# Moving projection steps from the middle of a recurrence to its end, in a hybrid RWKV-7 and latent-attention block

## The chip, the cores and the metric

The kernel runs on one core of a Trainium2 chip. The metric is the device time of one execution in microseconds; the comparison is between medians of several runs. PE is TensorE (PEld its weight loads), DVE VectorE, ACT ScalarE, POOL GpSimd and SP SyncE, which issues most DMAs.

## What is computed

One decoder layer over 1024 tokens of width 1024, all in float32. The input is normed and modulated, and one projection of 3360 columns feeds two groups. The first is an RWKV-7 recurrence of 8 heads of 64, the second a latent attention of 8 heads. Each result is multiplied by a gate from the same projection; both are joined, projected back, and added to the input. Cut to what matters:

```python
h = rms_norm(x, norm_g[l]) * (1 + scale[:, None, :]) + shift[:, None, :]
proj = h @ w_in[0]
y_rwkv, v_first = rwkv7_time_mix(proj[..., :SHIFT_WIDTH], ...)       # recurrence, then group norm per head
y_mla = mla_branch(proj[..., O_CQ:O_CKV], proj[..., O_CKV:O_KR], proj[..., O_KR:O_GM], ...)
y = concatenate([y_rwkv * silu(proj[..., O_GR:O_CQ]), y_mla * silu(proj[..., O_GM:])])
x = x + gate[:, None, :] * (y @ w_out[l])
return rms_norm(x, final_g)

def step(state, inp):                                                # of the recurrence
    sa = einsum('bhvk,bhk->bhv', state, kk_t)
    state = state * w_t - sa[..., None] * (kk_t * a_t) + v_t[..., None] * k_t
    y = einsum('bhvk,bhk->bhv', state, r_t)
```

## The kernel before

**Tiling.** Matrix products that need float32 accuracy are made of three matmuls, high by high, high by low and low by high, on operands split into a rounded part and a rest. The projection works in tiles of 128 output columns by 512 tokens; each takes 8 blocks of the contraction, three matmuls a block (`mm3`, L159 to L161). Such a block is one *step* of `proj` (L333), and a tile of 128 columns has 16 steps. Its results go through the two PSUM banks of `psM`.

**The recurrence** is cut into 8 units: 4 pairs of heads (p) by 2 halves of the sequence (h), each with 8 chunks of 64 tokens. For a unit, `prep` (L462) makes decayed keys, queries and values, `products` (L544) the products within a chunk, `invert` (L588) inverts the triangular matrices by 62 dependent operations on DVE and stores them through DRAM (`d_n`, `d_w`), `fetch` and `tmat` (L607, L621) build the matrix T. Then `chain` (L653) runs the 8 chunks in three slots each: X is copied by ACT (L672), T times X (L679) and the copied result go into ST (L685, L686), and the new state is written (L693, L694); Y collects the output (L676, L696). `post` (L700) is the group norm: a copy of Y (L705), a reduction (L707, L708), the subtraction on POOL (L709), squares on ACT (L712), a second reduction (L714, L715), the power and the product on POOL (L716, L717), transposes on PE (L723), the affine part on ACT (L726), and the sum, gate and store (L730 to L736).

**What sets the order.** A loop of 11 rounds (n = 0 to 10) weaves these together. Round n has STEPS[n] slots (j). It prepares unit n at the slots of PREP and PROD, builds T of unit n - 1, runs the chain of unit n - 2, one third of a chunk in each slot, and does the group norm of unit n - 3 in five pieces, at the slots of POST. In each slot RATE[n] is added to a debt, and for each whole unit of debt one step of the *filler* is issued. The filler (L913) goes through the 24 remaining projection tiles: keys, values and queries of the later units, the latents (`latent`, L349: three tiles for queries, two for keys and values), and the gates; then through `values` (L830), which makes the rotated queries (`qrope`), the value matrix Vt (L863 to L872) and keys and queries of the first head pair (`heads_qk`, L794). That is 428 steps in all. What the rounds leave is drained after the loop.

Two calls of `latents` (L818) load the projected latents back from DRAM and split them: the first one the query latents (SP issues them by L763, ACT and DVE split them), in round 7, the second one those of keys and values, in round 8. `values` starts only after both, and after all projections, because its tiles take the memory of the normed input.

The program is traced in this order; a scheduler then orders the instructions of each engine by priority, and each engine runs its own in that order. After the loop, attention begins with the scores (`scores`, L1013), whose first matmul is L1023.

Of the kernel before, what the change touches and what calls it, by code (L numbers as in the profile page):

```python
# [57 lines left out]
PREP = ((0, 0, 1, 2, 3, 5, 5, 7), (4, 4, 5, 6, 7, 9, 9, 11), (9, 9, 10, 11, 12, 14, 14, 16))  # L58
PROD = ((8, 13), (12, 15), (17, 21))
TURN = (2, 5, 6)  # L60
POST = (1, 1, 5, 5, 8)
TMAT = ((13, 15), (14, 15), (15, 17))
EVAC = 120
STEPS = (16, 16, 24, 24, 24, 24, 24, 24, 24, 24, 9)
RATE = (2.3, 2.3, 2, 2, 2.2, 2, 2, 2, 1.7, 0.4, 1)
SCALE = 96 ** -0.5

_COLS = [("c", 8), ("norm_g", 8), ("b_shift", 8), ("b_scale", 8), ("mu", 13), ("a0", 4), ("k_k", 4),
# [14 lines left out]
def hymba_kernel(ctx: ExitStack, tc: tile.TileContext, x, pos, cols, cst, winit, w_ada, b_gate, w_in, w_lora, w0,  # L83
# [460 lines left out]
    def products(un, q):  # L544

        p, h, kb, rq = un["p"], un["h"], un["kb"], un["rq"]
        pp = [psA.tile([P, 4, P], F32, tag="rp", name="gps") for _ in range(2)]
        for i in range(4):
            c = q * 4 + i
            for s in range(2):  # L550
                rows = slice(s * 64, s * 64 + 64)
                T.matmul(pp[s][:, i, :], lhsT=kb[rows, c, :, :].rearrange("p a t -> p (a t)"),  # L552
                         rhs=rq[rows, c, :, :].rearrange("p a t -> p (a t)"), start=True, stop=True)
        dn = d_n[2 * p + h][:].rearrange("(s q c b) i j -> s q b i c j", s=2, q=2, b=2)
        for s in range(2):
            mk = cs("m_b" if s else "m_a")
            ga = ch.tile([P, 4, P], F32, tag="GA", name="GA", bufs=CB["GA"])
            un["GA"][s][q] = ga
            V.tensor_tensor(ga[:], pp[s][:], mk[:, None, :].to_broadcast([P, 4, P]), ALU.mult)
            for b in range(2):  # L560
                rr = slice(s * 64 + b * 32, s * 64 + b * 32 + 32)
                SY.dma_start(dn[s, q, b], ga[rr, :, b * 32:b * 32 + 32])

    def alloc_b(un):
        un["KB"] = ch.tile([P, 2, 8, C], F32, tag="KB", name="KB", bufs=CB["KB"])
        un["ST"] = ch.tile([P, 8, 2, C], F32, tag="ST", name="ST", bufs=CB["ST"])

    def turn_kb(un):

        ps = [psA.tile([P, 8, C], F32, tag="rt", name="tps") for _ in range(2)]  # L570
        for c in range(8):
            for s in range(2):
                rows = slice(s * 64, s * 64 + 64)
                T.transpose(ps[s][:, c, :], un["kb"][rows, c, :, :].rearrange("p a t -> p (a t)"), ident[rows, rows])
        for s in range(2):
            A.activation(un["KB"][:, s], ps[s][:], AF.Copy, scale=col("hs_b" if s else "hs_a"))

    def turn_v(un, q):

        qs = slice(q * 4, q * 4 + 4)  # L580
        ps = psA.tile([64, 4, P], F32, tag="rt", name="vps")
        for i in range(4):
            c = q * 4 + i
            T.transpose(ps[:, i, :], un["v"][:, c * C:(c + 1) * C], ident)
        A.copy(un["ST"][64:128, qs, 0, :], ps[:, :, 0:64])
        A.copy(un["ST"][0:64, qs, 1, :], ps[:, :, 64:128])

    def invert(un):  # L588

        i = 2 * un["p"] + un["h"]  # L590
        N = ch.tile([P, 32, 32], F32, tag="N", name="N", bufs=CB["N"])
        for q in range(4):
            SY.dma_start(N[q * 32:(q + 1) * 32], d_n[i][:])
        W = ch.tile([P, 8, 32], F32, tag="W", name="W")
        SY.dma_start(W[:].rearrange("p i t -> p (i t)"), winit)
        tp = ch.tile([P, 128], F32, tag="wtmp", name="wtmp")
        for u in range(31):
            n, m = u // 4 + 1, 31 - u
            t = tp[:, :n * m].rearrange("p (i t) -> p i t", i=n)
            V.tensor_tensor(t, W[:, 0:n, u:u + 1].to_broadcast([P, n, m]),  # L600
                            N[:, u:u + 1, u + 1:32].to_broadcast([P, n, m]), ALU.mult)
            V.tensor_tensor(W[:, 0:n, u + 1:32], W[:, 0:n, u + 1:32], t, ALU.subtract)  # L602
        d = d_w[i][:].rearrange("n (i q) t -> q n i t", q=4)
        for q in range(4):
            SY.dma_start(d[q], W[q * 32:(q + 1) * 32])

    def fetch(un):  # L607

        i = 2 * un["p"] + un["h"]
        TT = un["TT"] = TTs[un["h"]]  # L610
        dw = d_w[i][:].rearrange("(s c b) i j -> s b i c j", s=2, b=2)
        W1 = ch.tile([P, 8, 32], F32, tag="W1", name="W1")
        T1 = un["T1"] = ch.tile([P, 8, 32], F32, tag="T1", name="T1")
        for s in range(2):
            a = s * 64
            SY.dma_start(W1[a:a + 32], dw[s, 0])
            SY.dma_start(TT[a + 32:a + 64, :, 32:64], dw[s, 1])
            SY.dma_start(TT[a:a + 32, :, 0:32], dw[s, 0])
            V.transpose(flat(T1)[a:a + 32], flat(W1)[a:a + 32])

    def tmat(un):  # L621

        GA, TT, T1 = un["GA"], un["TT"], un["T1"]
        ps = psA.tile([P, 8, 32], F32, tag="rt", name="y1ps")
        for c in range(8):
            for s in range(2):
                a = s * 64
                T.matmul(ps[a + 32:a + 64, c, :], lhsT=GA[s][c // 4][a:a + 32, c % 4, 32:64], rhs=T1[a:a + 32, c, :],
                         start=True, stop=True)
        Y1 = ch.tile([P, 8, 32], F32, tag="Y1", name="Y1")  # L630
        A.mul(Y1[32:64], ps[32:64], -1.0)
        V.tensor_scalar(Y1[96:128], ps[96:128], -1.0, None, ALU.mult)
        yield
        ps = psA.tile([P, 8, 32], F32, tag="rt", name="y2ps")
        for c in range(8):
            for s in range(2):
                a = s * 64
                T.matmul(ps[a:a + 32, c, :], lhsT=Y1[a + 32:a + 64, c, :], rhs=TT[a + 32:a + 64, c, 32:64],
                         start=True, stop=True)
        A.copy(TT[0:32, :, 32:64], ps[0:32])  # L640
        V.tensor_copy(TT[64:96, :, 32:64], ps[64:96])

        for q in range(2):
            A.copy(GA[0][q][0:64, :, 0:C], un["rq"][0:64, q * 4:q * 4 + 4, 0, :])
            A.copy(GA[1][q][64:128, :, 0:C], un["rq"][64:128, q * 4:q * 4 + 4, 0, :])
        yield
# [284 lines left out]
    def late(n):  # L931

        return 2 if 2 <= n <= 6 else int(n == 1)

    def after(n):

        at_ = {}

        def put(j, f):
            at_.setdefault(j, []).append(f)  # L940

        if n < 8:
            g = prep(units[n])
            for j in PREP[late(n)]:
                put(j, lambda g=g: next(g, None))
            for j, q in zip(PROD[late(n)], range(2)):
                put(j, lambda q=q: products(units[n], q))
            put(PROD[late(n)][1], lambda: invert(units[n]))
        if 1 <= n < 9:
            un = units[n - 1]  # L950
            put(0, lambda: alloc_b(un))
            put((1, 5, 11)[late(n - 1)], lambda: fetch(un))
            put(TURN[0], lambda: turn_kb(un))
            for j, q in zip(TURN[1:], range(2)):
                put(j, lambda q=q: turn_v(un, q))
            g2 = tmat(un)
            for j in TMAT[1 if n == 1 else late(n - 1) and 2]:
                put(j, lambda g2=g2: next(g2, None))
        if 3 <= n < 11:
            g3 = post(units[n - 3])  # L960
            for j in POST:
                put(j, lambda g3=g3: next(g3, None))
        return at_

# [3 lines left out]
    for n in range(11):  # L968
        at_ = after(n)
        rec = chain(units[n - 2], units[n - 1] if n % 2 == 0 else None) if 2 <= n < 10 else None  # L970
        for j in range(STEPS[n]):
            if rec is not None:
                next(rec, None)
            for f in at_.pop(j, ()):
                f()
            if (n, j) == (7, PREP[0][-1] + 1):
                next(la)
            if (n, j) == (8, TURN[2]):
                next(la)
                turned.append(1)  # L980
            debt += RATE[n]
            while debt >= 1:
                next(fill, None)
                debt -= 1
        assert not at_, at_.keys()
# [349 lines left out]
```

## Time and profile before

| what | us |
|---|---|
| median of three runs (lowest, highest) | 945.38 (942.20, 951.51) |
| the profiled execution: time; span from the first to the last instruction | 947.39; 945.6 |
| first X copies of the eight units, rounds 2 to 9 | 167.4, 228.6, 296.0, 358.1, 424.3, 493.7, 561.2, 606.6 |
| last projection matmul; first value matmul (L863) | 591.1; 607.6 |
| last Y matmul ends; last transposes L723; first scores L1023 | 648.3; 657.1; 664.7 |

How to read the views. A window row gives a stretch (start:end in us from the span's start), its length, the busy time and the number of instructions of PE, PEld, DVE, ACT and POOL, the share of the clock granted to PE, the mean busy share of the DMA engines, and GB/s. A row of waits gives who waited for whom, the sum in us, how many times, and the longest. A timeline row gives start, duration, engine, line, operation and operands; in brackets stands the idle time of its engine just before, and what ended it. A row of a group of instructions gives the line, the operation, its count, then busy us, mean ns of one, and idle time before. Matmuls overlap each other, so that a stream of them starts one more often than each lasts.

### The profile page before, as it was taken

Reading aid. Unit: us, or ns where it says so; the run is one execution under the profiler, and the core shown is the slowest. Engines: PE = TensorE matmul, PEld = TensorE weight load, DVE = VectorE, ACT = ScalarE, POOL = GpSimd, SP = SyncE. Lnnn points to the kernel's source line nnn. Section 1 sums busy time; section 2 is a strip of 40 time slices with the busy share of each in tenths; the row PEclk is TensorE's granted clock in tenths of the full one; section 3 lists DMA queues with packets and bytes.
Section 4 is the critical chain, followed back from the end, with each engine's and each line's share of the span. In section 5 each row is a group of like instructions: output and inputs, shape, how many; then the busy total and the mean of one; then the engine's idle time right before and its main releaser. Section 6 shows DMA issues by size and latency. Waiting matters only on the chain.

```text
span 945.6 us, 16387 instructions
## 1 busy us (share of the span) xinstructions
PE 850.4 (90%) x5828; PEld 638.6 (68%) x5828; DVE 576.5 (61%) x1438; ACT 476.7 (50%) x1132; POOL 294.1 (31%) x355
## 2 busy tenths in 40 slices
PE   1799998999889999999999899896899998989897
PEld 1587776776667567667776666663677777868685
DVE  5796484293863855936636736462678778764333
ACT  2656131535635535445435444564688788762311
POOL 2314131133222322412325130323346454464300
PEclk9999998799999999999999999797899999999899
DMA  8762313124413424232332543335202031026133
GB/s 270 228 183 73 84 29 87 57 68 107 143 37 98 138 68 124 72 81 86 90 85 63 140 123 87 113 103 150 54 26 71 26 101 57 1 89 223 56 115 130
DMA packets 116737, 93.01 MB, mean 98 GB/s; under 512 B 38952, under 2 KB 92464, under 8 KB 116656
## 3 DMA queue, kind: packets, MB, share of 16 engines
q1 hardware_dynamic: 115696, 88.82, 32.0%
q0 software_dynamic: 960, 3.15, 1.4%
q8 instruction: 46, 0.75, 0.3%
q14 instruction: 35, 0.29, 0.1%
HBM read 69.12 MB, written 22.81 MB: 97 GB/s over the span
## 4 chain that ended last, share of the span: by engine, by line
PE 54%; DVE 17%; ACT 9%; DMA 7%; issue 5%; POOL 5%; SPq 1%; POOLq 0%; DVEq 0%; ACTq 0%
PE mm L159 8%; PE mm L160 6%; PE mm L161 6%; DVE W L602 3%; DVE wtmp L600 3%; DMA wor<-in_w_out 2%; PE tp L1052 2%; ACT pr L1041 2%; PE gps L552 2%; PE po L1114 2%; PE po L1116 2%; PE po L1115 2%; PE Y L676 2%; ACT PTh L1061 1%; PE rc L668 1%
## 5 line engine op out<-in xcount | busy, mean ns | idle before, releaser
L159 PE MATMUL mm<-hTh,whi 128*128 128x512 f32 (+1 forms) x384 | 171.8, 447 | 1.9 <-DVE tg L230 1.9
L160 PE MATMUL mm<-hTl,whi 128*128 128x512 f32 (+1 forms) x384 | 154.2, 402 | 0.0
L161 PE MATMUL mm<-hTh,wlo 128*128 128x512 f32 (+1 forms) x384 | 154.2, 401 | 0.0
L152 POOL TENSOR_TENSOR wlo<-wraw,whi 128x512 fp32r<-128x512 f32 (+1 forms) x54 | 69.8, 1293 | 206.8 <-ACT whi L151 192.3
L159 PEld LDWEIGHTS mm<-hTh,whi 128*128 128x128 f32 (+1 forms) x384 | 72.3, 188 | 23.6 <-issue 2.3
L161 PEld LDWEIGHTS mm<-hTh,wlo 128*128 128x128 f32 (+1 forms) x384 | 72.3, 188 | 17.8
L160 PEld LDWEIGHTS mm<-hTl,whi 128*128 128x128 f32 (+1 forms) x384 | 72.8, 190 | 12.4 <-issue 1.4
L1045 POOL TENSOR_SCALAR pr<-pr,sm 128x512 f32<-128x512 f32 (+2 forms) x96 | 55.2, 584 | 77.4 <-DVE sm L1042 50.0
L602 DVE TENSOR_TENSOR W<-W,wtmp 128x60 f32<-128x60 f32 (+24 forms) x248 | 68.8, 277 | 6.0
L600 DVE TENSOR_TENSOR wtmp<-W,N 128x60 f32<-128x60 f32 (+24 forms) x248 | 66.1, 267 | 7.0 <-DMA N<-d_n 0.9
L1041 ACT ACTIVATE pr<-sp,mx,rss 128x128 f32<-128x128 f32 (+3 forms) x64 | 53.3, 833 | 15.4 <-DVE mx L1034 13.0
L1062 DVE TENSOR_TENSOR PTl<-tp,PTh 128x512 fp32r<-128x512 f32 (+2 forms) x96 | 52.4, 554 | 12.2 <-ACT PTh L1061 10.1
L151 ACT CAST whi<-wraw 128x512 fp32r<-128x512 f32 (+1 forms) x54 | 32.6, 605 | 51.6 <-PE mm L160 45.1
L1033 DVE TENSOR_REDUCE mx<-sp 128x1 f32<-128x128 f32 (+3 forms) x64 | 48.0, 750 | 13.4 <-PE sp L1027 13.3
L1114 PE MATMUL po<-wo,yh 128*128 128x512 f32 x128 | 51.7, 404 | 3.9 <-DVE xo L1247 3.1
L1061 ACT CAST PTh<-tp 128x512 fp32r<-128x512 f32 (+2 forms) x96 | 44.0, 477 | 14.4 <-PE tp L1052 10.6
L1115 PE MATMUL po<-wo,yh 128*128 128x512 f32 x128 | 51.2, 400 | 0.0
L1116 PE MATMUL po<-wo,yl 128*128 128x512 f32 x128 | 51.2, 400 | 0.0
L1052 PE MATMUL tp<-cstt,pr 128*128 128x128 f32 x288 | 44.9, 278 | 4.4 <-POOL pr L1045 2.1
L1073 PE MATMUL op<-PTh,Vt 128*128 128x256 f32 (+1 forms) x160 | 41.9, 292 | 5.1 <-ACT od L1088 5.1
L685 ACT ACTIVATE ST<-rc 64x64 f32<-64x64 f32 x64 | 13.8, 215 | 52.7 <-PE rc L682 44.7
L1023 PE MATMUL sp<-kt,qt 96*128 96x512 f32 (+2 forms) x96 | 36.4, 379 | 4.2 <-ACT pr L1041 4.2
(394 smaller groups left out, 1974.7 us busy)
## 6 DMA issues: line engine op xcount, KB each, us to landing
wraw<-in_w_in SPq DMA_DIRECT2D x52, 256.0 KB, 3.0
wa<-in_w_ada SPq DMA_DIRECT2D x64, 128.0 KB, 3.4
xt<-in_x SPq DMA_DIRECT2D x8, 512.0 KB, 5.8
wg<-in_w_ada SPq DMA_DIRECT2D x32, 128.0 KB, 2.2
N<-d_n SPq DMA_DIRECT2D x32, 128.0 KB, 2.8
wor<-in_w_out SPq DMA_DIRECT2D x16, 256.0 KB, 2.9
cr<-d_c SPq DMA_DIRECT2D x14, 256.0 KB, 2.8
d_c<-craw SPq DMA_DIRECT2D x10, 256.0 KB, 2.6
```

Source lines behind the costliest of these rows:

```text
L152: G.tensor_tensor(lo[:, :, :m], raw[:, :, :m], hi[:, :, :m].bitcast(F32), ALU.subtract)
L159: T.matmul(ps[:m], lhsT=hi[:, k % 4, :m], rhs=a, start=first, stop=False)
L160: T.matmul(ps[:m], lhsT=hi[:, k % 4, :m], rhs=b, start=False, stop=False)
L161: T.matmul(ps[:m], lhsT=lo[:, k % 4, :m], rhs=a, start=False, stop=last)
L600: V.tensor_tensor(t, W[:, 0:n, u:u + 1].to_broadcast([P, n, m]), N[:, u:u + 1, u + 1:32].to_broadcast([P, n, m]), ALU.mult)
L602: V.tensor_tensor(W[:, 0:n, u + 1:32], W[:, 0:n, u + 1:32], t, ALU.subtract)
L1041: A.activation(pr[:, 0:n], sp[:, 0:n], AF.Exp, scale=rss[:, i:i + 1], bias=mx[:], accum_out=sm[:])
L1045: G.tensor_scalar(pr[:, a:e], pr[:, a:e], sm[:], 1.0, ALU.mult, ALU.mult)
L1052: T.transpose(tp[:, j, :], pr[:, (j0 + j) * P:(j0 + j + 1) * P], ident)
L1114: T.matmul(ps, lhsT=yh[k][:, ts_], rhs=hi, start=first, stop=False)
L1115: T.matmul(ps, lhsT=yh[k][:, ts_], rhs=lo, start=False, stop=False)
L1116: T.matmul(ps, lhsT=yl[k][:, ts_], rhs=hi, start=False, stop=last)
```

## The change

Three tables of numbers and one slot are changed:

```diff
-POST = (1, 1, 5, 5, 8)
+POST = ((1, 1, 5, 5, 8), (0, 0, 9, 9, 13))
-STEPS = (16, 16, 24, 24, 24, 24, 24, 24, 24, 24, 9)
-RATE = (2.3, 2.3, 2, 2, 2.2, 2, 2, 2, 1.7, 0.4, 1)
+STEPS = (16, 16, 24, 24, 24, 24, 24, 24, 24, 24, 14)
+RATE = (2.3, 2.3, 1.8, 1.8, 1.9, 1.8, 1.8, 1.8, 1.75, 1.3, 1)
...
-            for j in POST:
+            for j in POST[n == 10]:
                 put(j, lambda g3=g3: next(g3, None))
...
-            if (n, j) == (7, PREP[0][-1] + 1):
+            if (n, j) == (7, 16):
                 next(la)
```

Rounds 2 to 7 issue fewer steps in a slot, round 9 more, and round 10, which holds only the last unit's group norm, has 14 slots instead of 9; that norm's transposes come at slot 9 and not 5. The query latents are loaded at slot 16 of round 7 and not at slot 8.

In the built order this moves instructions at three places. On PE, from the last Y matmul of the last unit (L696) on: `ytps` are the norm's transposes, `vps` value blocks, `qkps` keys and queries of the first head pair. Before:

```order
L696 MATMUL Y<-ST,GA 64x64 x2
L787 MATMUL qkps<-ckvh_6000,wkl 128x512
L723 MATMUL ytps<-cstt,ys 64x128 x8
L785 MATMUL qkps<-cqh_5411,wqh 128x512
L786 MATMUL qkps<-cql_5414,wqh 128x512
L787 MATMUL qkps<-cqh_5411,wql 128x512
```

With the change (four value blocks and a rotated query's block stand where the dots are):

```order
L696 MATMUL Y<-ST,GA 64x64 x2
L863 MATMUL vps<-wvh,ckvh_5868 128x512
L864 MATMUL vps<-wvl,ckvh_5868 128x512
...
L864 MATMUL vps<-wvl,ckvh_5869 128x512
L865 MATMUL vps<-wvh,ckvl_5871 128x512
L723 MATMUL ytps<-cstt,ys 64x128 x8
L785 MATMUL qkps<-ckvh_5868,wkh 128x512
L786 MATMUL qkps<-ckvl_5870,wkh 128x512
```

33 matmuls of 512 columns stand between the last Y matmul and the transposes, where one stood, and 30 between the transposes and the first scores, where 18 stood.

On DVE, between the two reductions of the last unit's norm (L707 and L714). Before:

```order
L707 TENSOR_REDUCE s_6599<-ys 128x8
L805 TENSOR_TENSOR kt_6648<-qkps,kt_6648 64x512
L708 TENSOR_SCALAR s_6599<-s_6599 128x8
L753 TENSOR_TENSOR wkl<-wkr,wkh 128x128 x2
L805 TENSOR_TENSOR kt_6648<-qkps,kt_6648 64x512
L714 TENSOR_REDUCE s_6605<-y_6603 128x8
```

With the change:

```order
L707 TENSOR_REDUCE s_6549<-ys 128x8
L872 TENSOR_TENSOR Vt<-vps,Vt 128x4x128
L436 TENSOR_TENSOR rl<-q_6515,rh 128x512
L708 TENSOR_SCALAR s_6549<-s_6549 128x8
L424 STREAM_SHUFFLE rot<-q_6575 128x512
L431 TENSOR_TENSOR q_6575<-q_6575,tabs 128x512
L431 TENSOR_TENSOR rot<-rot,tabs 128x512
L872 TENSOR_TENSOR Vt<-vps,Vt 128x4x128
L432 TENSOR_TENSOR q_6575<-q_6575,rot 128x512
L872 TENSOR_TENSOR Vt<-vps,Vt 128x4x128
L714 TENSOR_REDUCE s_6555<-y_6553 128x8
```

Splits of values (L872) and the last rotation of queries (L424 to L436) have come between the reductions.

On SP, around the stores and loads of the last unit's inversion (`d_n_99`); L763 loads the query latents. Before:

```order
L562 DMA d_n_99<-GA 32x4x32 x4
L763 DMA cr<-d_c_87 128x512
L763 DMA cr<-d_c_88 128x512
L763 DMA cr<-d_c_86 128x512
L150 DMA wraw<-in_w_in 128x4x128
L763 DMA cr<-d_c_87 128x512
L763 DMA cr<-d_c_88 128x512
L605 DMA d_w_106<-W 256x1x32 x4
L774 DMA wqr<-in_w_uqr 128x128 x3
L562 DMA d_n_99<-GA 32x4x32
```

With the change:

```order
L562 DMA d_n_99<-GA 32x4x32 x4
L605 DMA d_w_106<-W 256x1x32 x4
L562 DMA d_n_99<-GA 32x4x32 x4
...
L593 DMA N<-d_n_99 32x1024 x4
L595 DMA W<-in_winit 128x256
L763 DMA cr<-d_c_86 128x512
L763 DMA cr<-d_c_87 128x512
```

All loads of query latents now stand behind the inversion's own stores and loads.

## The prediction

> **What bounds the kernel now.** I read the busy time by stage first (windows cut at the first copy of X of a unit), then the waits of PE, then the timeline around the longest of them.
>
> ```profile
> core 0: us, PE busy (x) PEld busy (x) DVE busy (x) ACT busy (x) POOL busy (x), PEclk, DMA share, GB/s
> 296.00:358.10 62.10, 59.42 (x512) 38.71 (x510) 40.87 (x106) 31.49 (x86) 18.52 (x18) 1.00 0.40 112
> 358.10:424.30 66.20, 64.10 (x496) 45.97 (x494) 41.72 (x112) 29.00 (x76) 18.81 (x17) 1.00 0.32 88
> 591.10:607.60 16.50, 14.01 (x170) 10.09 (x170) 4.65 (x13) 9.94 (x31) 2.56 (x6) 0.78 0.44 135
> 607.60:648.90 41.30, 39.34 (x264) 25.98 (x263) 22.07 (x42) 23.65 (x66) 11.12 (x14) 0.92 0.34 96
> 648.90:657.10 8.20, 0.01 (x1) 0.01 (x1) 3.79 (x9) 2.54 (x6) 4.99 (x6) 0.65 0.55 183
> ```
>
> PE bounds the recurrence: in rounds 4 and 5 of the loop (296 to 424 us) it is busy for 96% and 97%, and between 607.6 and 648.9 us for 95%. The exception is 648.9 to 657.1 us, right after the last unit's recurrence, where PE does nothing. The waits of PE, from 167 to 591 us and then from 591 to 680 us (total, times, longest), say the same:
>
> ```profile
> PE rc L668 <- ACT ST L694: 4.9, 5, 2.1
> PE gps L552 <- DVE bv L539: 2.8, 2, 2.0
> PE mm L159 <- DVE tg L230: 1.9, 2, 1.4
> ```
>
> ```profile
> PE ytps L723 <- POOL ys L717: 8.2, 1, 8.2
> PE qkps L785 <- DVE qt L805: 2.5, 1, 2.5
> PE rc L679 <- ACT X L672: 1.8, 1, 1.8
> ```
>
> The first list is thin for 424 us; the second is led by one wait of 8.2 us. In the timeline it is the group norm of the last unit, a chain over ACT, DVE and POOL:
>
> ```profile
> 648.67 0.58 ACT L705 COPY ys<-Y 128x512 f32<-128x512 f32 x1
> ...
> 649.30 0.68 DVE L707 TENSOR_REDUCE s<-ys 128x8 f32<-128x512 f32 x1
> ...
> 650.62 0.15 DVE L708 TENSOR_SCALAR s<-s 128x8 f32<-128x8 f32 x1
> ...
> 652.76 0.69 DVE L714 TENSOR_REDUCE s<-y 128x8 f32<-128x512 f32 x1 [0.73 <-ACT y L712]
> ...
> 655.98 1.05 POOL L717 TENSOR_TENSOR ys<-ys,s 128x512 f32<-128x512 f32 x1
> ...
> 657.09 1.92 PE L723 MATMUL ytps<-cstt,ys 128*64 128x128 f32 x8 [8.23 <-POOL ys L717]
> ```
>
> From the copy of Y (648.67) to the end of the last product (657.03) it takes 8.4 us. The transposes are next in PE's program, so the 18 query matmuls behind them wait too.
>
> **The change part by part.** No work is removed or added; projection steps change places. A step is three matmuls of 512 columns, and two of these start 0.23 us apart at full clock:
>
> ```profile
> 663.51 0.39 PE L786 MATMUL qkps<-cql,wqh 128*128 128x512 f32 x1
> 663.74 0.39 PE L787 MATMUL qkps<-cqh,wql 128*128 128x512 f32 x1
> ```
>
> So a step is 0.70 us of PE. By slots times rate, rounds 2 to 7 issue 292.8 steps before and 261.6 now: 31.2 fewer, 21.8 us. Round 8 gets 1.2 of them, round 9 21.6, round 10 5.0, the drain after the loop 3.4. In the built order 63 such matmuls, not 19, stand between the last unit's final Y matmul and the first scores. Where PE is the bound at both ends, the move itself costs nothing, and only what PE loses by waits and by its clock can change. I sum these losses against the profiled execution's span, 945.6 us. Its time, 947.39, lies 2.0 over the median of the runs, 945.38; I take the difference off the median.
>
> *The wait before the last transposes.* One matmul covered the norm; now 33 do, 33 x 0.233 = 7.7 us. But the norm gets longer. Between its two reductions DVE now has nine other instructions: three splits of values, a shuffle, four tensor operations of the rotation, and the small L708.
>
> ```profile
> L872 DVE TENSOR_TENSOR Vt<-vps,Vt 128x512 fp32r<-128x512 f32 x8 | 5.4, 688 | 5.4 <-ACT Vt L871 5.4
> ...
> L424 DVE STREAM_SHUFFLE rot<-q 128x512 f32<-128x512 f32 x4 | 2.9, 732 | 0.0
> ```
>
> At 0.69 us for a full tile, 0.73 for the shuffle and 0.15 for L708 they are 7 x 0.69 + 0.73 + 0.15 = 5.7 us. L707 to L714 then takes 0.7 + 5.7 = 6.4 us against 3.5 now: 2.9 more. POOL also works beside a busy DVE; the unit before, in the same position, shows the price, 1.32 against 1.05 us for L717, and L709 will pay as much:
>
> ```profile
> 607.54 1.43 POOL L709 TENSOR_TENSOR ys<-ys,s 128x512 f32<-128x512 f32 x1 [8.53 <-DVE s L708]
> ...
> 612.77 1.32 POOL L717 TENSOR_TENSOR ys<-ys,s 128x512 f32<-128x512 f32 x1
> ```
>
> That is 0.5 together, and I add one DVE tile, 0.7, because DVE may be in the rotation when Y is copied. So 8.4 + 2.9 + 0.5 + 0.7 = 12.5 us of norm stand against 7.7 of cover: 4.8 of wait are left, 3.4 saved. Bounds: 0 to 8.2 saved.
>
> *The clock behind it.* After a wait PE runs at half its clock for a while:
>
> ```profile
> 600.20:610.40 10.20, 9.13 (x108) 7.27 (x108) 4.02 (x9) 6.81 (x20) 1.43 (x1) 0.50 0.11 35
> 617.00:618.90 1.90, 0.11 (x3) 0.07 (x4) 0.89 (x2) 1.90 (x6) 0.91 (x3) 1.00 0.03 11
> 620.70:624.10 3.40, 3.40 (x10) 2.65 (x9) 1.33 (x5) 2.11 (x5) 1.07 (x1) 0.50 0.84 248
> 651.40:661.60 10.20, 4.14 (x13) 3.08 (x14) 1.49 (x3) 2.87 (x5) 5.50 (x7) 0.50 0.60 152
> ```
>
> From 651.4 to 661.6 us PE worked 4.1 us at half clock, so 2.1 were lost. A wait of only 1.8 us at 617 was followed by 3.4 us at 0.50, so I expect the same behind 4.8 us: 0 saved, bounds 0 to 2.1.
>
> [...]
>
> *The wait of 1.8 us for X* and its 3.4 us at half clock (1.7 lost) came from value and rotation work queued on ACT ahead of L672. Most of this work now stands behind the recurrence, but a cast of a weight stands ahead of the last X and casts of values ahead of two copies into ST. At about 0.6 us for a cast of a full tile (below) I put 1.3 on these: 3.5 - 1.3 = 2.2 saved, bounds -1 to 3.5.
>
> *From the last projection to the first value matmul* PE has only recurrence and nine query matmuls, while the value weights are loaded:
>
> ```profile
> 597.59 1.43 POOL L777 TENSOR_SCALAR wvr<-wvr,colt 128x512 f32<-128x512 f32 x2 [1.08 <-DMA wvr<-in_w_v]
> ...
> 606.73 0.62 ACT L750 CAST wvh<-wvr 128x512 fp32r<-128x512 f32 x1
> ```
>
> The weights were scaled at 599.0 us and cast only at 606.7, behind the last unit's T matrix (L628 to L645) and a norm's copy. In the change that T matrix stands among projections of round 8, and three chunks of recurrence fill the load instead of four. The half clock of 600 us is to be expected again. I take 0.8 saved; bounds -2 to 3.7 (2.5 us without PE up to 607.6, and 1.2 on the first six matmuls at half clock).
>
> *After the transposes* four blocks of keys and queries follow, not two. A block's copy takes four turns of ACT and DVE, 2.6 us, on two banks, and the rope rows of the first queries are now issued by POOL behind L732:
>
> ```profile
> 659.37 0.80 PE L785 MATMUL qkps<-cqh,wqh 128*128 128x512 f32 x1 [0.37 <-ACT y L726]
> ...
> 662.31 1.29 POOL L732 TENSOR_TENSOR y<-bv,y 128x512 f32<-128x512 f32 x1 [4.23 <-DMA bv<-d_bv]
> ...
> 662.80 0.58 ACT L804 CAST qt<-qkps 64x512 fp32r<-64x512 f32 x1 [2.32 <-PE qkps L787]
> ...
> 664.74 0.69 DVE L805 TENSOR_TENSOR qt<-qkps,qt 64x512 fp32r<-64x512 f32 x1 [0.65 <-ACT qt L804]
> ```
>
> ```profile
> qt<-d_qr POOLq DMA_DIRECT2D x4, 256.0 KB, 3.8
> ```
>
> PE alone needs 2.3 us (657.1 to 659.4) and 30 x 0.233 = 7.0: 9.3 from the transposes to the scores. The rope rows need 5.2 us to L732, 1.3 for it, 0.5 for the first of two issues, and 3.8 to land: 10.8. The third block, waiting for the first one's bank, adds 1.2 to PE, which lies inside that. 1.5 lost, bounds 0 to 4.
>
> *Rounds 2 to 7 with fewer steps, and the latents* loaded eight slots later, behind the last unit's block stores and not among them: I take 0, since PE is the bound there. Bounds: 4.8 saved, if all three waits between 500 and 545 us go, to 14 lost (the third rival).
>
> ```profile
> PE gps L552 <- DVE W L602: 1.7, 1, 1.7
> PE rc L668 <- ACT ST L694: 1.7, 1, 1.7
> PE mm L159 <- DVE tg L230: 1.4, 1, 1.4
> ```
>
> The sum: 3.4 + 0 + 2.2 + 0.8 - 1.5 + 0 = 4.9 us saved, 945.4 - 4.9 = **940.5 us**. That is half a per cent; 1%, 9.5 us, is about what a measurement of this kernel can tell from no change.
>
> **The rivals.**
>
> *The norm is covered whole.* If DVE gets to L714 within the cover, the wait of 8.2 and the 2.1 of half clock go: 8.2 + 2.1 + 2.2 + 0.8 - 1.5 = 11.8 saved, 933.6 us. For it: 7.7 us of cover are nearly the 8.4 of the norm as it is. Against it: the nine instructions between the reductions. [...]
>
> *The latents' loads were what delayed the last preparation.* The three waits between 500 and 545 us vanish: 4.9 + 4.8 = 9.7 saved, 935.7 us. For it: in SP's queue the loads stand among the stores on which the inversion waits. Against it: two of the three name work of DVE and ACT that the change does not touch.
>
> *The rounds do not shrink (slower).* If rounds 2 to 7 are paced by preparation, inversion and the DMAs between them, taking steps out only opens gaps, and the steps cost their full time where they land. For it are the steps of rounds 4 and 5, by their first matmul:
>
> ```profile
> L159 PE MATMUL mm<-hTh,whi 128*128 128x512 f32 (+1 forms) x39 | 17.0, 435 | 0.0
> L159 PE MATMUL mm<-hTh,whi 128*128 128x512 f32 x56 | 24.7, 441 | 0.0
> ```
>
> 17 more steps, 11.9 us of PE, made the round only 4.1 us longer (62.1 to 66.2). Against it: round 4 has other work as well, and PE was busy for 96% of it. If a share f of the 21.8 us does not come back, the change costs 21.8 f - 4.9; it decides from f = 0.22. With the share that the two rounds show, f = 1 - 4.1 / 11.9 = 0.65, it is 14.2 - 4.9 = 9.3 lost: 954.7 us.
>
> *The wait only moves.* The norm's wait shrinks, and as much is lost in front of the first scores: 945 us.
>
> **How the numbers follow.** Chances: the forecast 0.42, the covered norm 0.15, the latents 0.17, the rounds that do not shrink 0.18, the wait that moves 0.08. The forecast's own range is 936 to 946. For 8 in 10 I go from 931, below the covered norm, to 953, which leaves out about half of the slow rival. Faster by over 1% (below 935.9): 0.15, half of the latents' 0.17 and 0.07 from the forecast's edge, 0.31. Slower by over 1% (above 954.8): half of the slow rival and a little, 0.11. The rest, 0.58, lies within 1%.
>
> **What would show it.** In the changed profile the wait of L723 on L717 should be 3 to 6 us, with half clock behind it; PE's first value matmul should come about 10 us after the last projection; rounds 2 to 7 together should be about 20 us shorter than now; no wait of PE between the last unit's chunks should exceed 1 us. The forecast is wrong if rounds 2 to 7 shrink by less than 15 us, if L723 waits as long as before or not at all, or if a wait of several us stands before the first L1023.

## The result and the profile after

The change makes the kernel slower: 957.90 us (median of 4 runs, 951.72 to 963.17) against 946.31, a ratio of 1.0104 with a 95% interval of 1.0059 to 1.0148. 940.5 had been forecast; the range ended at 953. The profiled execution of the change took 963.17 us, its span is 961.4, so it is 5 us above the median; that of before, 947.39, lies 1 us above its own.

The span is 15.8 us longer. To see where, I cut both traces at the first X copy of unit 0, the first of unit 6, the last of unit 7, and the first scores. First the kernel before, then the change:

```profile
167.40:561.20 393.80, 378.39 (x3002) 266.55 (x3000) 233.04 (x643) 186.25 (x479) 108.88 (x103) 0.97 0.33 92
561.20:646.30 85.10, 79.13 (x628) 53.76 (x629) 47.05 (x126) 47.19 (x134) 19.62 (x24) 0.92 0.36 106
646.30:664.70 18.40, 9.80 (x42) 6.87 (x43) 5.37 (x11) 7.39 (x17) 8.36 (x11) 0.72 0.50 138
664.70:945.60 280.90, 252.16 (x1435) 209.10 (x1433) 181.37 (x401) 167.42 (x392) 113.18 (x169) 0.97 0.25 80
```

```profile
169.10:551.20 382.10, 370.14 (x2907) 257.41 (x2905) 220.39 (x628) 176.40 (x460) 103.98 (x95) 0.95 0.31 86
551.20:613.80 62.60, 59.53 (x426) 41.94 (x426) 32.61 (x95) 32.28 (x85) 13.95 (x13) 0.84 0.32 93
613.80:649.90 36.10, 34.05 (x247) 23.31 (x248) 12.75 (x26) 18.44 (x58) 12.95 (x16) 0.91 0.35 116
649.90:682.50 32.60, 25.33 (x98) 18.57 (x98) 17.06 (x34) 13.87 (x27) 10.24 (x14) 0.84 0.63 171
682.50:961.40 278.90, 250.77 (x1435) 207.70 (x1433) 180.61 (x400) 167.69 (x392) 112.59 (x167) 0.97 0.24 77
```

The second row of before covers units 6 and 7; in the change these are the second and third. Rounds 2 to 7 (the first row) lost 97 projection matmuls of 512 columns, 841 to 744 by the traces' records, which is 22 us, but became only 11.7 us shorter. Units 6 and 7 took in 42 of them (10 us) and became 13.6 us longer; the stretch up to the first scores took in 55 (13 us) and became 14.2 us longer. (Ahead of the first row the change is 1.7 us longer, in the last 2.0 shorter.) So the steps cost their price or more where they landed, and gave back half of it where they left. The third number from the right is the granted clock: it fell from 0.97 to 0.95 in the rounds and to 0.84 in unit 6.

In the rounds PE waits less than before, not more: its idle times over 0.1 us sum to 11.7 us, 15.4 before. From 169 to 552 us the three longest groups of waits are

```profile
PE gps L552 <- DVE W L602: 3.8, 3, 1.7
PE bps L536 <- DVE kw L528: 1.9, 1, 1.9
PE rc L668 <- ACT ST L694: 1.3, 2, 0.9
```

The end went nearly as forecast. The norm (timeline, 654.69 to 667.74) took 13.1 us, and L723 waited 4.2:

```profile
654.69 0.59 ACT L705 COPY ys<-Y 128x512 f32<-128x512 f32 x1
...
663.02 0.67 DVE L714 TENSOR_REDUCE s<-y 128x8 f32<-128x512 f32 x1
...
666.69 1.05 POOL L717 TENSOR_TENSOR ys<-ys,s 128x512 f32<-128x512 f32 x1
...
667.80 1.91 PE L723 MATMUL ytps<-cstt,ys 128*64 128x128 f32 x8 [4.18 <-POOL ys L717]
```

The waits of PE from the last projection to after the first scores follow. The second and third stand behind the transposes:

```profile
PE ytps L723 <- POOL ys L717: 4.2, 1, 4.2
PE sp L1023 <- ACT pr L1041: 1.8, 1, 1.8
PE qkps L785 <- DVE kt L805: 1.8, 1, 1.8
PE Y L676 <- ACT ST L693: 1.0, 3, 0.5
```

New in the change is a hole at the start of unit 6. Its first three chunks stand in PE's order without a single projection matmul, and 66 stand in the fourth; from 550.3 to 569.0 us none starts. Two windows of the change:

```profile
554.50:569.00 14.50, 12.31 (x88) 8.32 (x88) 11.72 (x35) 11.94 (x34) 5.37 (x6) 0.50 0.32 88
569.00:575.00 6.00, 6.00 (x15) 4.72 (x15) 5.41 (x23) 1.70 (x4) 0.18 (x1) 0.50 0.48 172
```

PE is busy for 85% of the first, in no wait of more than 0.53 us, and runs at half clock all the same. The first projection matmuls behind the hole run at half clock too. The half clock lasts 20.5 us, from 554.5 to 575.0.

### The profile page after: what moved, and what is told of

Read it like the earlier page. It is cut to its first block, busy times and chain, and to the rows that moved or that the text cites. A ratio compares the mean times of both kernels' runs of the same rounds, so it can differ in the third digit from the quotient of the medians.

```text
span 961.4 us, 16404 instructions
## 1 busy us (share of the span) xinstructions
PE 874.4 (91%) x5828; PEld 654.0 (68%) x5828; DVE 573.3 (60%) x1438; ACT 477.3 (50%) x1132; POOL 297.7 (31%) x355
## 4 chain that ended last, share of the span: by engine, by line
PE 55%; DVE 19%; ACT 9%; issue 6%; DMA 5%; POOL 5%; SPq 1%; POOLq 0%; DVEq 0%; ACTq 0%
PE mm L159 9%; PE mm L160 7%; PE mm L161 7%; DVE W L602 3%; DVE wtmp L600 3%; ACT pr L1041 2%; PE gps L552 2%; DMA wor<-in_w_out 2%; ACT PTh L1061 2%; PE tp L1052 2%; PE po L1114 2%; PE Y L676 2%; PE po L1116 2%; PE po L1115 2%; PE rc L668 2%
## 5 line engine op out<-in xcount | busy, mean ns | idle before, releaser
L159 PE MATMUL mm<-hTh,whi 128*128 128x512 f32 (+1 forms) x384 | 175.6, 457 | 0.1
L160 PE MATMUL mm<-hTl,whi 128*128 128x512 f32 (+1 forms) x384 | 157.4, 410 | 0.0
L161 PE MATMUL mm<-hTh,wlo 128*128 128x512 f32 (+1 forms) x384 | 157.3, 410 | 0.0
L600 DVE TENSOR_TENSOR wtmp<-W,N 128x60 f32<-128x60 f32 (+24 forms) x248 | 69.1, 278 | 7.2 <-DMA N<-d_n 1.8
L1062 DVE TENSOR_TENSOR PTl<-tp,PTh 128x512 fp32r<-128x512 f32 (+2 forms) x96 | 52.2, 553 | 11.7 <-ACT PTh L1061 9.9
L672 ACT COPY X<-rc 128x64 f32<-128x64 f32 x64 | 13.5, 211 | 56.6 <-PE rc L668 56.0
```

Source lines behind the costliest of these rows:

```text
L159: T.matmul(ps[:m], lhsT=hi[:, k % 4, :m], rhs=a, start=first, stop=False)
L160: T.matmul(ps[:m], lhsT=hi[:, k % 4, :m], rhs=b, start=False, stop=False)
L161: T.matmul(ps[:m], lhsT=lo[:, k % 4, :m], rhs=a, start=False, stop=last)
```

## The experiments

All times are compared with the kernel before on the same chip.

| kernel | median us | ratio to before, 95% interval |
|---|---|---|
| the change | 957.90 | 1.0104 [1.0059, 1.0148] |
| late_latents | 948.14 | 1.0051 [1.0026, 1.0077] |
| latents11 | 956.18 | 1.0153 [1.0103, 1.0202] |
| rates_alone | 956.66 | 1.0133 [1.0099, 1.0168] |
| end_alone | 939.82 | 0.9945 [0.9915, 0.9975] |
| padded | 963.39 | 1.0181 [1.0141, 1.0221] |
| mild_rates | 952.16 | 1.0073 [1.0044, 1.0102] |
| beside_last | 941.33 | 0.9929 [0.9902, 0.9956] |
| one_step_early | 953.48 | 1.0081 [1.0046, 1.0117] |
| one_step_late | 951.41 | 1.0049 [1.0025, 1.0072] |
| change_early | 968.56 | 1.0261 [1.0231, 1.0292] |
| change_late | 973.18 | 1.0324 [1.0283, 1.0365] |
| end_early | 949.62 | 1.0055 [1.0026, 1.0083] |
| end_late | 947.24 | 1.0023 [0.9995, 1.0052] |

### The change taken apart

The first theory was the hole (H), its rival the slow rival of the prediction (R). Three parts can be made alone, and one put back.

**late_latents**: the kernel before, and

```diff
-            if (n, j) == (7, PREP[0][-1] + 1):
+            if (n, j) == (7, 16):
```

> The kernel before with one edit: the query latents are loaded at slot 16 of round 7 and not at slot 8. Rates, rounds and norm stay. Theory H (hole): with the load at slot 16 the built order of PE leaves the first chunks of unit 6 without any projection matmul (0, 0, then 45 of 512 columns in three chunks, where it was 15, 15, 15), so few columns pass through PE there, its clock falls to half for 10 to 20 us, and the kernel becomes 3 to 9 us slower, 949 to 955 us. Theory R (the rounds do not shrink, as in the prediction's slow rival): the place of the load does not matter, 946 us, and unit 6 keeps its length.

1.0051: the hole alone costs 4.8 us. It stands in the trace as expected, and behind it this stretch at half clock:

```profile
568.90:579.10 10.20, 8.77 (x43) 6.41 (x42) 8.04 (x26) 6.60 (x19) 4.46 (x6) 0.50 0.27 88
```

**latents11**: the change, and

```diff
-            if (n, j) == (7, 16):
+            if (n, j) == (7, 11):
```

> The changed kernel with one edit: the query latents at slot 11 of round 7, where the built order has no empty chunk in unit 6 (15 or more matmuls of 512 columns in each). Theory H: the 20.5 us of half clock at the start of unit 6 go, 8 to 12 us come back, 945 to 950 us; unit 6 becomes 8 to 12 us shorter. Theory R: rounds 2 to 7 with fewer steps are what costs, so it stays at 955 to 960 us.

The hole and its half clock went, and unit 6 became 10.3 us shorter (52.3 against 62.6), as H said:

```profile
554.70:607.00 52.30, 50.03 (x407) 33.32 (x405) 27.97 (x84) 25.73 (x71) 12.48 (x10) 1.00 0.32 93
```

But the time did not come back: 1.0153, which cannot be told from the change's 1.0104. Unit 5 before it took 69.2 us instead of 62.3: 6.8 us of it ran at half clock, where the change has none there, and PE sat idle for 3.5 us instead of 1.0. The splits of the latents now stand in that unit on ACT and DVE (L750 and L753, 3.7 and 4.4 us); that they are the reason is not shown. H is not the main cause.

**rates_alone**: the kernel before with the rates of the change up to round 9,

```diff
-RATE = (2.3, 2.3, 2, 2, 2.2, 2, 2, 2, 1.7, 0.4, 1)
+RATE = (2.3, 2.3, 1.8, 1.8, 1.9, 1.8, 1.8, 1.8, 1.75, 1.3, 1)
-            if (n, j) == (7, PREP[0][-1] + 1):
+            if (n, j) == (7, 11):
```

> The kernel before with the rates of the change in rounds 2 to 9, the query latents at slot 11 of round 7 (the earliest place at which they are projected by then), and the group norm's slots and the length of round 10 as before. Theory H: what the rates alone cost is small, within 5 us of before (942 to 951 us), since no new hole stands in the order. Theory R: the moved steps cost 14 us of rounds that do not shrink, 953 to 960 us.

1.0133: R's value. The rates are the costly part (the edit also moves the latents by three slots).

**end_alone**: the kernel before with the norm's slots and the 14 slots of round 10,

```diff
-POST = (1, 1, 5, 5, 8)
-STEPS = (16, 16, 24, 24, 24, 24, 24, 24, 24, 24, 9)
+POST = ((1, 1, 5, 5, 8), (0, 0, 9, 9, 13))
+STEPS = (16, 16, 24, 24, 24, 24, 24, 24, 24, 24, 14)
-            for j in POST:
+            for j in POST[n == 10]:
```

> The kernel before with only the end changed: 14 slots in round 10 and the last unit's group norm at slots 0, 0, 9, 9, 13. Rates and latents stay. In the built order the norm's transposes then stand behind the first scores of the attention, so nothing waits for the norm. Both theories: the wait of 8.2 us and the half clock behind it go, part of it is lost again to waits for the copies of keys and queries (2 to 4 us), so 3 to 7 us are saved, 939 to 943 us. If the norm's end is needed soon after by the gate and the store, nothing is saved, 946 us.

0.9945, 5 us faster, the best part of the change. Its waits of PE from 649 us on:

```profile
PE sp L1023 <- DMA qt<-d_qr: 3.9, 1, 3.9
PE sp L1025 <- DVE qt L805: 1.0, 1, 1.0
PE qkps L785 <- DVE kt L805: 0.7, 1, 0.7
PE ytps L723 <- POOL ys L717: 0.6, 1, 0.6
```

The wait of 8.2 us on L717 is 0.6, because the first scores now stand ahead of the transposes; half of it came back as a wait for the rope rows of the queries, the DMA behind POOL's queue that the prediction had priced.

The three parts sum to 0.51 + 1.33 - 0.55 = 1.29%, the whole is 1.04%: they add up within the intervals.

### What sets the half clock

**gate** measures the clock by itself; the kernel's body is replaced by turns of PE and ACT:

```diff
+    def group(n, k=P):
+        nonlocal cur
+        ps = pp.tile([P, HALF], F32, tag="ps", name="ps", bufs=2)
+        while n > 0:
+            m = min(n, HALF)
+            T.matmul(ps[:, :m], lhsT=cur[:k], rhs=xr[:k, HALF:HALF + m], start=True, stop=True)
+            n -= m
+        nxt = sb.tile([P, P], F32R, tag="cur", name="cur", bufs=2)
+        A.activation(nxt[:], ps[:, :P], AF.Copy, scale=0.0884)
+        cur = nxt
+    for n in GROUPS:
+        group(60 * HALF)
+        for _ in range(int(41 / (0.8 + n / 2400))):
+            group(n)
...
```

> Not the reference's computation: a measurement of the clock alone. PE and ACT take turns: PE issues matmuls of n columns in all, ACT copies 128 columns of the result, the next matmuls take that copy as weights. n is 256, 384, 512, 640, 768, 896, 1024, 1280, some 40 us each, each time after 60 dense matmuls of 512 columns, and once more for the last six after a thin stretch. [...] Theory I (idle): half clock follows only a wait of PE of one to several us; no wait here exceeds 1 us, so the clock stays full at every n.

The theory against I was C: the clock goes by the columns that pass in a window, with full clock expected from n = 896 on. A turn took longer than I had estimated for that, 0.9 us at n = 256 and 1.5 at 1280, so the loads were thinner. All n up to 1024 fell to half clock within two windows of 3.41 us, also 896 and 1024. At n = 1280 the full clock held for five windows of 3000 to 3770 columns and fell behind one of 3150; the two rows are the time before and after. The waits of PE from 402 to 512 us stand below them (total, times, longest):

```profile
466.80:483.90 17.10, 11.28 (x42) 6.39 (x40) 0.00 (x0) 3.61 (x13) 0.00 (x0) 1.00 0.00 0
487.30:511.10 23.80, 18.25 (x40) 10.39 (x39) 0.00 (x0) 3.61 (x13) 0.00 (x0) 0.50 0.00 0
```

```profile
PE ps L102 <- ACT cur L105: 26.3, 61, 0.7
```

No wait exceeds 0.7 us, and the clock falls: theory I, that only a long wait costs clock, is wrong.

**gate_states** repeats it at higher loads, after a dense and after a thin start (GROUPS = 1408 to 3072, all of them in both loops).

> Not the reference's computation: the measurement of the clock again, with n = 1408, 1536, 1792, 2048, 2560 and 3072 columns a turn, each once after 60 dense matmuls and once after 16 thin turns of 128 columns. In the first measurement windows of 3.41 us with 3000 columns or more kept the full clock and those under 3000 mostly lost it, and a turn took about 0.7 us beside its columns. Theory C (columns in a window): after the dense start every n from 1408 on keeps the full clock (3.413 x n / (0.7 + n / 2400) is 3700 columns a window and more); after the thin start the columns pass at half speed, 3.413 x n / (0.7 + n / 1200) is 2570 at 1408 and 2900 at 2048, so these stay at half clock for good, and only 2560 and 3072 (3080 and 3220) come back. The same turns then run at two speeds by what went before. Rival: the clock depends on the load alone, so both starts end at the same clock after a few windows.

Of the two rates in these sums the traces bear out one: at half clock matmuls of 512 columns start 0.43 us apart (before, 484.54 to 486.25 us), 1200 columns a us. 2400 is twice that, and no run shows it: at full clock they start 0.225 to 0.235 us apart in the same trace, 2180 to 2280 a us.

At n = 1536 after the dense start 27 turns took 37 us, and after the thin one as many took 57 us, at half clock to the end; n = 1792 did the same. The rows are n = 1536, dense start and thin start:

```profile
84.00:121.00 37.00, 25.61 (x81) 12.81 (x79) 0.00 (x0) 7.40 (x27) 0.00 (x0) 1.00 0.00 0
418.00:475.00 57.00, 45.47 (x84) 22.95 (x84) 0.00 (x0) 7.48 (x27) 0.00 (x0) 0.50 0.00 0
```

Two values missed: 1408 fell after 25 us from the dense start, and 2048 came back from the thin one. The same work thus runs at either speed, by what went before: at half clock fewer columns pass in a window (2480 at n = 1536 where 3830 pass at full clock, by 27 turns in 57 and in 37 us), and the clock stayed at 0.50.

The traces of the 15 versions of the whole kernel agree. All changes of the clock lie on a grid of 3.413 us, within 0.03. I added up the columns that passed in each grid window at full clock (each matmul's columns from its start on), and counted what came next:

| columns in the window | windows | followed by half clock |
|---|---|---|
| under 2000 | 104 | 103 |
| 2000 to 2500 | 36 | 33 |
| 2500 to 3000 | 81 | 35 |
| 3000 to 3500 | 139 | 12 |
| 3500 to 4000 | 167 | 4 |
| over 4000 | 3122 | 0 |

Where a matmul on the edge of a window is counted moves single counts by up to six. Dense matmuls pass about 7700 (512 every 0.225 to 0.235 us). So the limit lies near 2700 columns, a third, but it is not sharp: in gate and gate_states windows of some 3100 to 3200 columns were followed by half clock (n = 1024, 1280 and 1408), and one of 3000 was not. The four of 3500 to 4000 all start at 163 to 166 us, among 67 to 76 matmuls, mostly of 64 rows or fewer; weighted by their rows, of 128, these count 1700 to 1800. Over all windows the columns weighted so divide about as well as the plain ones, so it stays open whether a matmul of 64 rows counts whole. A *busy* PE is no protection: of the 187 windows ahead of a half clock PE was busy over 95% in 18. Three windows of the kernel before: one with a wait, one with PE busy all the time, and the one behind that:

```profile
272.50:276.00 3.50, 1.28 (x15) 0.84 (x14) 3.09 (x8) 1.27 (x3) 0.00 (x0) 0.99 0.06 9
...
480.80:484.20 3.40, 3.40 (x33) 2.74 (x30) 0.83 (x1) 1.94 (x6) 1.26 (x1) 1.00 0.35 79
484.20:487.60 3.40, 3.40 (x12) 2.14 (x11) 0.64 (x3) 0.00 (x0) 1.01 (x1) 0.50 0.37 127
```

The groups of PE in the second, by form, show why: one matmul of 512 columns, the rest of 128, 64 or 1:

```profile
L552 PE MATMUL gps<-rq,kb 64*128 64x128 f32 x12 | 1.7, 314 | 0.0
L360 PE MATMUL lps<-colt,csq 128*128 128x1 f32 x8 | 1.1, 253 | 0.0
L159 PE MATMUL mm<-hTh,whi 128*128 128x512 f32 x1 | 0.7, 679 | 0.0
```

**padded**: does the clock explain the rounds? latents11, with three matmuls of no use ahead of each half of a projection tile in rounds 2 to 7:

```diff
...
+                if 2 <= at_round[0] <= 7:
+                    for k in range(3):
+                        T.matmul(ps[:m], lhsT=hTh[k][:, :m], rhs=hTh[k][:, HALF:], start=True, stop=True)
                 for k in range(NK):
                     mm3(ps, m, w, slice(h * HALF, (h + 1) * HALF), k, k == 0, k == NK - 1)
```

> The changed kernel with the query latents at slot 11 of round 7, and in rounds 2 to 7 each half of a projection tile begins with three more matmuls of 512 columns whose result the first real one overwrites: some 95 matmuls without use, about as many columns as the change took out of these rounds, 22 us of PE. Theory C (the missing columns halve the clock): the half clock in units 0 to 5 goes back from 20 to 26 us of excess to 13 to 16, so the rounds grow by 12 to 15 us only and the kernel takes 968 to 972 us. Theory P (a step costs its full time there, the half clock is chance): the rounds grow by 20 to 23 us, 976 to 980 us. Theory R (preparation sets the pace of the rounds and the added matmuls fill waits): 956 to 964 us, and the clock does not matter.

Rounds 2 to 7 of the two profiled executions, latents11 and then padded:

```profile
169.30:554.70 385.40, 370.08 (x2924) 257.60 (x2922) 227.12 (x639) 182.11 (x473) 104.67 (x98) 0.95 0.32 88
164.60:565.10 400.50, 386.77 (x3019) 271.48 (x3017) 234.25 (x642) 183.66 (x473) 106.34 (x99) 0.95 0.31 84
```

96 matmuls of no use, 22 us of PE, cost 3 us by the ratios (1.0181 against 1.0153, whose intervals overlap) and 6 us by the medians, each taken over the kernel before on its own chip: R's range, below C's. In the profiled executions the rounds grew by 15.1 us, but the profiled latents11 was the fastest of its runs. So the added work cost between an eighth and two thirds of its price: it filled time that was empty of columns. C is not shown for these rounds. The mean granted clock of whole runs rose from 0.955 to 0.963, back to that of the kernel before (0.960), but the rounds of the two traces have about as much half clock (38 and 41 us).

### A version in between, and a null test

**mild_rates**: the end of the change, with

```diff
+RATE = (2.3, 2.3, 1.95, 1.95, 2.2, 1.95, 1.95, 1.95, 1.7, 0.87, 1)
```

> A version that may beat both: the norm's slots and the 14 slots of round 10 as in the change, query latents at slot 8 as before, and rates of 1.95 in rounds 2, 3, 5, 6 and 7, 2.2 in round 4, 1.7 in round 8, 0.87 in round 9. In the built order no chunk of unit 6 is then without projection matmuls (15, 15, 12, 18, 15, 18, 6, 13 where before has 15, 15, 15, 15, 16, 5, 0, 0). Theory C: less half clock in units 2 and 6, about 4 us better than the end of the norm alone, 933 to 938 us. Theory R (each step taken out of rounds 2 to 7 costs half its price): six steps fewer there cost about 2 us, 940 to 944 us.

1.0073, worse than both theories allow: six steps fewer in rounds 2 to 7, and eleven more beside the last unit, cost 1.3% against end_alone. The amount alone can't do that. A new theory (S) was needed: the built order itself is sensitive.

**beside_last**: end_alone with a rate of 0.87 in round 9 (before 0.4), so that eleven steps stand beside the last unit and not behind it.

> The end of the change alone (14 slots in round 10, norm at slots 0, 0, 9, 9, 13; it took 939.8 us) with a rate of 0.87 in round 9 and not 0.4: eleven steps that stood after the last unit now stand beside it; rounds 2 to 8 as before. If steps beside the last unit are hidden in its chain's waits, 4 to 7 us are saved against that run, 933 to 936 us. If PE is the bound there too, they cost the same in both places, 938 to 941 us. Theory S: slower by some waits, 942 to 948 us.

0.9929 against 0.9945: the same. Such steps cost beside the last unit what they cost behind it, so the loss of mild_rates is not theirs.

**one_step_early**, **one_step_late**: the kernel before with

```diff
-    debt = 0.0
+    debt = 1.0
```

and with -1.0.

> The kernel before with the debt of steps started at 1 and not at 0: every projection step comes one step earlier in the program, nothing else. Rates, norm, latents as before. Theory C (the amount of steps in rounds 2 to 7 decides, through the clock): the amounts do not change, so within 2 us of before, 942 to 946 us. Theory S (the built order is so sensitive that any new order costs some waits of a few us, whichever way the steps move): up to 1% away, most likely slower, 948 to 954 us.

> The same with the debt started at -1: every projection step one step later. Theory C: 942 to 946 us. Theory S: 948 to 954 us, and not by the same amount as one step early.

1.0081 and 1.0049: with as many steps in each of rounds 2 to 7 the kernel becomes 5 to 8 us slower either way. S holds: the order of the kernel before is the fastest of its three. It leaves open whether the change's 1% is anything else.

**change_early**, **change_late**, **end_early**, **end_late**: the same two edits in the change, and in end_alone.

> The changed kernel with the debt of steps started at 1: every projection step one step earlier. One step early and one step late cost the kernel before 0.8 and 0.5%, with nothing moved between rounds. Theory A (amount: the change is slower because the steps stand in other rounds): both shifts of the change stay at least 0.8% over before and 3 to 10 us over the shifted kernels of before, 954 to 964 us. Theory S (the change is slower only because its order is another, unlucky one): its shifted versions scatter around the shifted ones of before, 945 to 955 us, one of them below 951.

> The changed kernel with the debt started at -1. Theory A: 954 to 964 us, as one step early. Theory S: 945 to 955 us, on average with the other one about 952.

> The end of the change alone (it saved 0.55% against before) with every step one step earlier. If the saving at the end does not depend on the order elsewhere, it is 0.4 to 0.7% under the kernel before with the same shift, which took 1.008 times before: 1.001 to 1.004, 945 to 951 us. Theory S for the end too: the saving itself is luck, 1.005 to 1.010, 950 to 956 us.

> The end of the change alone with every step one step later. Not by luck: 0.4 to 0.7% under the kernel before with that shift, which took 1.005 times before: 0.998 to 1.001, 942 to 949 us. By luck: 1.003 to 1.008, 948 to 954 us.

Theory A, by more than it said: 1.0261 and 1.0324. At the same shift the change is 1.0, 1.8 and 2.7% slower than the kernel before, 1.9% or 18 us on the mean, so its own order was a lucky one. The end alone is 0.55, 0.26 and 0.26% faster than before at the same shift: it saves 2 to 5 us, though the two later intervals overlap those of before. In the traces, rounds 2 to 7 one step early, first before and then the change:

```profile
172.60:568.20 395.60, 379.03 (x3000) 266.99 (x3000) 233.41 (x643) 184.54 (x477) 110.13 (x102) 0.97 0.33 91
```

```profile
171.80:560.30 388.50, 376.74 (x2906) 260.01 (x2906) 216.25 (x627) 179.17 (x460) 102.94 (x95) 0.95 0.31 84
```

And one step late:

```profile
162.80:566.60 403.80, 384.22 (x3010) 271.06 (x3010) 228.95 (x646) 186.92 (x480) 109.75 (x104) 0.95 0.33 90
```

```profile
165.30:559.60 394.30, 378.15 (x2917) 262.21 (x2917) 211.53 (x632) 177.65 (x462) 106.51 (x97) 0.94 0.31 85
```

The rounds become 11.7, 7.1 and 9.5 us shorter, 9.4 on the mean, for some 22 us of matmuls taken out.

## Why the prediction was wrong

**The bound** was misread. PE was busy for 96% of the rounds, but busy is not full. A matmul of 64 columns lasts 0.22 to 0.27 us in the trace of before at full clock (L668), and at the pace of dense matmuls, 7700 columns in 3.413 us, its columns need 0.03. With that price I split rounds 2 to 7 into the time that their columns need at full clock, what those that start at half clock need more, and the rest, in which no column passes (estimates from one trace each, us):

| rounds 2 to 7 | length | columns | more at half clock | no column passes | of it PE busy |
|---|---|---|---|---|---|
| before | 393.8 | 259.4 | 9.2 | 125.2 | 109.8 |
| the change | 382.1 | 237.4 | 13.4 | 131.3 | 119.3 |
| one_step_early | 395.6 | 259.5 | 9.8 | 126.3 | 109.7 |
| change_early | 388.5 | 237.2 | 15.5 | 135.8 | 124.0 |
| one_step_late | 403.8 | 259.6 | 15.5 | 128.6 | 109.1 |
| change_late | 394.3 | 238.6 | 15.2 | 140.6 | 124.4 |
| latents11 | 385.4 | 238.5 | 12.9 | 134.0 | 118.7 |
| padded | 400.5 | 260.3 | 15.4 | 124.9 | 111.1 |

So columns filled two thirds of the rounds, and a third was the recurrence's short matmuls and waits.

**The failed step** is "Rounds 2 to 7 with fewer steps, and the latents": I took 0, since PE is the bound there, with a bound of 14 lost. It measured 10.1 in the profiled execution (11.7 shorter, not 21.8) and some 12 on the mean of the three orders (9.4, not 22), and the hole came on top, some 10 more in the profiled execution. The table shows where the 22 us went: 6.1, 9.5 and 12.0 us came back as time in which no column passes, and 4.2, 5.7 and -0.3 as columns at half clock. The first part is not idle time, which fell by 3.4 to 4.8 us; it is time that PE counts as busy. This is 109 to 112 us in all eight traces with the rates of before (late_latents, end_alone, beside_last and the two shifted ends are the other five) and 118 to 124 in the five with the change's (rates_alone is the fifth), and padded's useless matmuls brought it back to 111. The wide matmuls had passed their columns while the short ones lasted; taken out, they left much of that time behind, empty.

The slow rival thus named the right place and nearly the right size: f is 1 - 11.7 / 21.8 = 0.46 to 1 - 7.1 / 21.8 = 0.67 where it said 0.65. That its 954.7 us comes so near has luck in it, since it leaves the hole out. Its mechanism is borne out in part: steps taken out did leave time empty, but inside PE's busy time and not as gaps, and none of these runs shows that preparation or DMAs set the pace.

The clock has a part as well. In rounds 2 to 7 the eight traces with the rates of before show half clock for 24 to 41 us, the five with the change's for 38 to 48; short matmuls last longer in it too (0.34 us for L668 in the trace of before). If all work takes twice as long there, half of the added half clock is lost: 8.4, 8.2 and 3.5 us in the three pairs, as an upper estimate. Over whole runs, the mean granted clock is 0.960, 0.955 and 0.960 before, and 0.952, 0.947 and 0.945 in the change; time x (1 - clock) grows by 11 us on the mean. Over 89 runs of the kernel before, each us of that goes with 0.73 us of time (correlation 0.86). So about 8 of the 18 us between the two go with the clock. That few columns cost clock is shown in general (gate, and the windows); that the steps taken out of these rounds cost it is likely, and not shown, since padded's rounds kept their half clock.

The latents were the other half of the same step. The hole that their later load makes costs 4.8 us in the kernel before; in the change, removing it gained 10.3 us in unit 6, lost 6.9 in unit 5, and showed in no median.

**The end** was right in its terms. L723 waited 4.2 us (4.8 forecast), the norm took 13.1 (12.5), and 6.8 us of half clock followed. The first value matmul came 9.9 us after the last projection (about 10). No wait between the last unit's chunks exceeds 0.5 us, and none of several us stands ahead of the first scores. After the transposes 1.8 us were lost to a copy of keys, where 1.5 had been put on rope rows; these were in time. The X wait fell from 1.8 us to 0.2, but its half clock only moved: during and behind two chunks with 3 and 0 matmuls of 512 columns in unit 7 PE ran at half clock for 6.8 us, so its 2.2 were not saved in full. From unit 6 to the first scores the change took 27.8 us more for 22.6 us of steps. Some 10 of these are the hole, by what unit 6 gained without it, so the rest came out about 5 us ahead, as the 4.9 forecast; since single terms differ, this match has luck in it.

Of the indicators, the rounds were the one that failed: 11.7 us shorter, where 15 was the limit for the forecast.

The prediction read half clock as what follows a wait. A long wait is not needed for it: in gate no wait exceeds 0.7 us from 402 to 512 us, and 46.7 us of that (n = 1024, 401.9 to 448.6) ran at 0.50.

## What to carry to other kernels

Read a busy PE by the columns that its matmuls pass, and not by its busy share. Here wide matmuls had filled time in which short ones kept PE busy and passed little, so taking out 22 us of them gave back half. And the clock halved where the columns in 3.4 us fell under about a third of the full stream (behind 136 of the 140 windows under 2500 of some 7700), for the wide work too (0.43 us from one matmul of 512 columns to the next, 0.23 at full clock). Moving such work to where it fills a visible wait (8.2 us here) can therefore cost more than the wait, by many small losses that no list of waits shows. And before a gain or loss of 1% is put down to an idea, shift the whole order by one step without the idea: here that alone moved the time by 0.5 to 0.8%, so the change has to be compared over several orders.

The part worth keeping is the end alone: 0.9945 with the order as it is, and 0.9929 with eleven steps beside the last unit. Both beat the kernel before and the change; with the order shifted by a step the end alone gained 0.26%, within the noise.

## What was not expected of the hardware

The clock of TensorE changed only on a grid of 3.413 us in these traces, within 0.03. A window of under 2500 columns was nearly always followed by half clock (136 of 140) and one of over 3500 hardly ever (4 of 3289), whether PE waited in it (1.28 us busy of 3.5 at 272.5 us, some 1100 columns) or not (3.40 of 3.40 at 480.8, some 2300). Half clock lasted under work that kept full clock: at n = 1536 in gate_states 27 equal turns took 37 us at 1.00 or 57 us at 0.50, by the state in which they began. The grid's offset from the first instruction differs from trace to trace (2.9 us in that of before, 1.5 in that of the change); that it also differs between executions of one program is likely, and not shown, with one trace of each. Of the scatter of before's runs, 937 to 953 us, most goes with the granted clock (correlation 0.86).
